# Nearest 2x upsampling on one core: the last of three loads grows from 6 to 8 KB per partition, and SyncE instead of GpSimd ends the program

## The chip, the cores and the metric

The kernel runs on one core of one Trainium2 chip. The time is device time in microseconds (us), lower is better. Beside it stands the *span* of a profile, which goes from the start of the first to the end of the last of the program's own instructions; every timed run has both. The profile calls VectorE DVE, ScalarE ACT, GpSimd POOL, TensorE PE and SyncE SP. Engines and DMAs report progress by *semaphores*, counters that other engines wait for; a DMA has *landed* when its last semaphore step has been made. All runs quoted were at a granted clock of 1.0. A ratio is the mean time of one kernel's runs over that of the other's of the same rounds, so it is not quite the ratio of the medians that stand beside it.

## The reference

```python
batch, channels, h, w = (16, 64, 64, 64)          # float32
result[:, :, i, j] = x[:, :, i // 2, j // 2]      # 128 x 128 out
```

16.78 MB come in, 67.11 MB go out, and there is no arithmetic. Each of the 128 partitions holds 512 rows of 64 floats (128 KB in, 512 KB out).

## The kernel before

Three loads, issued at once by SyncE, bring everything into SBUF. Ten groups of rows are then expanded by VectorE (9/16 of each) and ScalarE, and each group is stored with one DMA.

```python
rows = [40, 44, 44, 54, 54, 56, 56, 56, 56, 52]      # rows per store, sum 512
cuts = [0, R // 2, R - 24, R]                        # loads of 256, 232 and 24 rows
loads = [nc.sync.dma_start(out=xt[:, lo:hi], in_=xp[:, lo:hi])
         for lo, hi in zip(cuts, cuts[1:])]
...
for n, k in enumerate(rows):
    ...
    nc.vector.tensor_copy(out=u[:, :kv], in_=expanded(r0, r0 + kv))
    nc.scalar.copy(out=u[:, kv:], in_=expanded(r0 + kv, r0 + k))
    store = nc.sync.dma_start(out=op[:, r0 : r0 + k, :], in_=u)
    if n == 0:
        tc.add_manual_dep(store.ins, loads[-2].ins.name, ...,
                          reason="stores begin as the loads end")
```

The first store needs only rows of the first load, but is held until the second load (`loads[-2]`) has landed. A row is 256 bytes per partition, so the loads are 64, 58 and 6 KB per partition. Each value is written four times, so a store of 56 rows has 56 KB per partition. In the trace every DMA is 128 data packets, one for each partition, and each of the 16 DMA engines moves eight of them: load packets are 64, 58 and 6 KB here, store packets 40 to 56 KB.

The end of the program was already rearranged. GpSimd (POOL in the profile) waits for all landings, the last store's included, clears the semaphores, and only then releases the other engines:

```python
blocks[-1].instructions = others + [
    d0, gather0, release0, gather1, d1, landed, clear, d2, release1
]
```

Of the kernel before, what the change touches and what calls it, by code (L numbers as in the profile page):

```python
# [1 line left out]

# [4 lines left out]



EARLY = 1  # L10


def begin_before_barrier(nc):



    blocks = nc.main_func.blocks
    main, body = blocks[0], blocks[1]
    sp = mybir.EngineType.SP
    loads = [i for i in body.instructions if i.engine == sp][:EARLY]  # L20
    for load in loads:
        assert isinstance(load, mybir.InstDMACopy), type(load)
        assert not (load.sync_info and load.sync_info.on_wait)
    names = [i.name for i in loads]
    body.instructions = [i for i in body.instructions if i.name not in names]
    kept = list(main.instructions)
    at = next(
        n
        for n, i in enumerate(kept)
        if i.engine == sp and isinstance(i, mybir.InstDrain)  # L30
    )
    kept[at:at] = loads
    main.instructions = kept


def close_on_gpsimd(nc):



    blocks = nc.main_func.blocks  # L40
    sp, pool = mybir.EngineType.SP, mybir.EngineType.Pool
    stores = [
        i
        for i in blocks[1].instructions
        if i.engine == sp and isinstance(i, mybir.InstDMACopy)
    ]
    last = stores[-1].sync_info.on_update[0].id

    end = list(blocks[-1].instructions)
    wait = end[0]  # L50
    assert wait.engine == sp and isinstance(wait, mybir.InstDrain)
    waits = sorted(wait.sync_info.on_wait, key=lambda w: w.id != last)
    assert waits[0].id == last and len(waits) > 2

    mine = [i for i in end if i.engine == pool]
    kinds = [type(i).__name__ for i in mine]
    assert kinds == [
        "InstDrain",
        "InstEventSemaphore",
        "InstEventSemaphore",  # L60
        "InstDrain",
        "InstISA",
        "InstDrain",
        "InstEventSemaphore",
        "InstEventSemaphore",
    ], kinds
    d0, gather0, release0, d1, clear, d2, gather1, release1 = mine
    landed = mybir.InstDrain(
        name=wait.name,
        engine=pool,  # L70
        debug=wait.debug,
        sync_info=mybir.SyncInfo(on_wait=waits, on_update=[]),
    )
    others = [i for i in end if i.engine != pool and i is not wait]
    blocks[-1].instructions = others + [
        d0, gather0, release0, gather1, d1, landed, clear, d2, release1
    ]


@with_exitstack  # L80
def kernel(
    ctx: ExitStack,
    tc: tile.TileContext,
    x: bass.AP,
    scale_factor: int,
    out: bass.AP,
):
    nc = tc.nc
    nc.at_finalize(begin_before_barrier)
    nc.at_finalize(close_on_gpsimd)  # L90
    P = nc.NUM_PARTITIONS
    s = int(scale_factor)
    B, C, H, W = x.shape
    R = B * C * H // P
    fdt = x.dtype



    xp = x.rearrange("b c h w -> (b c h) w").rearrange("(p r) w -> p r w", p=P)
    op = out.rearrange("b c (h hd) w -> (b c h) (hd w)", hd=s).rearrange(  # L100
        "(p r) w -> p r w", p=P
    )




    rows = [40, 44, 44, 54, 54, 56, 56, 56, 56, 52]
    GROW = s * s
    FREE = 79
    WF = FREE * GROW * W  # L110
    assert sum(rows) == R
    mem_pool = ctx.enter_context(tc.tile_pool(name="mem", bufs=1))
    mem = mem_pool.tile([P, WF + R * W], fdt, name="mem")
    xt = mem[:, WF:].rearrange("p (r w) -> p r w", r=R)



    cuts = [0, R // 2, R - 24, R]
    loads = [
        nc.sync.dma_start(out=xt[:, lo:hi], in_=xp[:, lo:hi])  # L120
        for lo, hi in zip(cuts, cuts[1:])
    ]

    def expanded(r0, r1):
        return (
            xt[:, r0:r1].unsqueeze(2).unsqueeze(4).to_broadcast([P, r1 - r0, s, W, s])
        )

    r0 = 0
    before = (0, 0)  # L130
    for n, k in enumerate(rows):
        size = k * GROW * W
        at = 0 if n % 2 == 0 else WF + r0 * W - size
        assert at >= before[1] or at + size <= before[0]
        before = (at, at + size)
        u = mem[:, at : at + size].rearrange(
            "p (k a w b) -> p k a w b", k=k, a=s, w=W
        )
        kv = k * 9 // 16
# [4 lines that stand above are left out]
            tc.add_manual_dep(  # L144
                store.ins,
                loads[-2].ins.name,
                mybir.DependencyInfo(
                    mybir.DependencyClass.Sync, mybir.DependencyReason.DATA
                ),
                reason="stores begin as the loads end",  # L150
            )
        r0 += k


# [1 line left out]
_INS = ['x', 'scale_factor']  # L156
_OUTS = [((16, 64, 128, 128), 'float32')]

_NUMBERS = {'scale_factor': 2}


# [26 lines left out]
```

## Time and profile before

| | before |
|---|---|
| median time | 198.72 us (198.65 to 198.76, 6 runs) |
| span of the profiled run | 196.92 us |
| time minus span | 1.78 us |
| DMA engines holding a packet | 99.0% of the span |
| DVE, ACT busy | 30%, 26% |
| last data packet ends | 196.20 us |
| last store's last semaphore step ("last landing") | 196.54 us |

The DMA engines are full and the compute engines mostly wait for buffers; the chain of waits is made of DMA to 71%. The last two rows come from the trace's packet and semaphore records. Those records do not name a packet's DMA engine; where this text speaks of one engine, packets were paired that follow one another within a few ns.

### The profile page before, as it was taken

To read this page: it belongs to the slowest core of one execution; us is meant where nothing else is said; L and a number is where in the kernel's file an instruction comes from. 1 tells how busy PE (TensorE), PEld (TensorE's weight loads), DVE (VectorE), ACT (ScalarE), POOL (GpSimd) and SP (SyncE) were. 2 spreads that over 40 slices of the span, in tenths; PEclk is the share of its full clock that TensorE was granted. 3 is DMA by queue.
4 is the path that set the end of the run, shared out by engine and by line. 5 is a ranking of instruction groups with operands and counts; after the bars stand their busy time and mean duration, and the time that the engine had idled before them with its cause. 6 is when DMAs were issued, how large, how long until landed. Compare 5 with 4: busy or idle time off the path is not lost.

```text
span 196.9 us, 104 instructions
## 1 busy us (share of the span) xinstructions
DVE 59.6 (30%) x10; ACT 52.1 (26%) x11; POOL 0.2 (0%) x4
## 2 busy tenths in 40 slices
DVE  0000570000050340610393096059119506900000
ACT  2000591000170360695000093800019460000000
POOL 0000000000000000000000000000000000000000
DMA  9999889699999999998989989889989989989995
GB/s 426 426 426 426 386 386 567 274 490 399 413 439 439 439 439 439 461 438 359 539 359 483 422 373 547 384 373 524 408 373 478 454 373 443 489 373 457 422 443 249
DMA packets 1872, 83.89 MB, mean 426 GB/s; under 512 B 208, under 2 KB 208, under 8 KB 336
## 3 DMA queue, kind: packets, MB, share of 16 engines
q1 hardware_dynamic: 1872, 83.89, 99.0%
HBM read 16.78 MB, written 67.11 MB: 426 GB/s over the span
## 4 chain that ended last, share of the span: by engine, by line
DMA 71%; DVE 13%; ACT 3%; issue 0%; SPq 0%; DVEq 0%; ACTq 0%
DMA out_dram<-mem 51%; DMA mem<-in_x_dram 20%; DVE mem L140 13%; ACT mem L141 3%; SPq L142 0%; DVEq L140 0%; ACTq L141 0%
## 5 line engine op out<-in xcount | busy, mean ns | idle before, releaser
L140 DVE COPY mem<-mem 128x7936 f32<-128x7936 f32 (+4 forms) x10 | 59.6, 5969 | 112.2 <-DMA out_dram<-mem 90.4
L141 ACT COPY mem<-mem 128x6400 f32<-128x6400 f32 (+4 forms) x10 | 50.8, 5077 | 107.8 <-DMA out_dram<-mem 81.8
L141 ACT ACT_TABLE_LOAD x1 | 1.3, 1283 | 0.8 <-PEq L169 0.8
L169 POOL MEMSET const-bfloat16-1.0<- 128x1 bf16 x1 | 0.1, 101 | 0.0
L169 POOL MEMSET const-uint8-127<- 128x1 uint8 x1 | 0.1, 101 | 0.0
L169 POOL MEMSET const-float32-0.0<- 128x1 f32 x1 | 0.1, 98 | 0.2 <-issue 0.2
L169 POOL MEMSET const-float32-1.0<- 128x1 f32 x1 | 0.1, 98 | 0.0
## 6 DMA issues: line engine op xcount, KB each, us to landing
out_dram<-mem SPq DMA_DIRECT2D x4, 7168.0 KB, 25.3
out_dram<-mem SPq DMA_DIRECT2D x2, 6912.0 KB, 25.8
out_dram<-mem SPq DMA_DIRECT2D x2, 5632.0 KB, 24.6
mem<-in_x_dram SPq DMA_DIRECT2D x1, 7424.0 KB, 38.6
out_dram<-mem SPq DMA_DIRECT2D x1, 6656.0 KB, 24.6
out_dram<-mem SPq DMA_DIRECT2D x1, 5120.0 KB, 14.1
mem<-in_x_dram SPq DMA_DIRECT2D x1, 768.0 KB, 40.1
mem<-in_x_dram SPq DMA_DIRECT2D x1, 21.9
```

What stands on the lines that cost most here:

```text
L140: nc.vector.tensor_copy(out=u[:, :kv], in_=expanded(r0, r0 + kv))
L141: nc.scalar.copy(out=u[:, kv:], in_=expanded(r0 + kv, r0 + k))
L169: nc = _bacc.Bacc("TRN2", target_bir_lowering=False, num_devices=1)
```

## The change

The intent is to give the DMA queue its first store before it runs dry, by letting the load that releases it land sooner, and to leave as little as possible to do after the last store's landing.

```diff
-    cuts = [0, R // 2, R - 24, R]
+    cuts = [0, R // 2, R - 32, R]
...
-    nc.at_finalize(close_on_gpsimd)
+    nc.at_finalize(close_early)
```

and in the new `close_early` (cut to its core, with `InstDrain` and `InstEventSemaphore` shortened):

```diff
+    lo, hi = clear.ant_dict["range_first"], clear.ant_dict["range_last"]
+    clears = []
+    for a, b in ((lo, last), (last + 1, hi + 1)):       # all but the last store's semaphore
+        if a < b:
+            clears.append(nc.gpsimd.sem_clear(range(a, b)).ins)
...
+    landed = InstDrain(engine=pool, on_wait=[w for w in waits if w.id != last])
+    final = InstEventSemaphore(engine=sp, on_wait=[w], on_update=[subtract w.wait_value])
-        d0, gather0, release0, gather1, d1, landed, clear, d2, release1
+        d0, gather0, release0, gather1, release1, d1, landed, *clears, d2, final
```

More of the change, by code (lines that the diff above doesn't have):

```diff
@@ L77, in close_on_gpsimd, with close_early @@
     ]
+def close_early(nc):
+    blocks = nc.main_func.blocks
+    sp, pool = mybir.EngineType.SP, mybir.EngineType.Pool
+    stores = [
+        i
+        for i in blocks[1].instructions
+        if i.engine == sp and isinstance(i, mybir.InstDMACopy)
+    ]
+    last = stores[-1].sync_info.on_update[0].id
+    end = list(blocks[-1].instructions)
+    wait = end[0]
+    assert wait.engine == sp and isinstance(wait, mybir.InstDrain)
+    waits = list(wait.sync_info.on_wait)
+    assert len({w.id for w in waits}) == len(waits) > 2
+    assert all(w.wait_mode == "sem-ge-imm" for w in waits)
+    mine = [i for i in end if i.engine == pool]
+    kinds = [type(i).__name__ for i in mine]
+    assert kinds == [
+        "InstDrain",
+        "InstEventSemaphore",
+        "InstEventSemaphore",
+        "InstDrain",
+        "InstISA",
+        "InstDrain",
+        "InstEventSemaphore",
+        "InstEventSemaphore",
+    ], kinds
+    d0, gather0, release0, d1, clear, d2, gather1, release1 = mine
+    lo, hi = clear.ant_dict["range_first"], clear.ant_dict["range_last"]
+    assert lo <= last <= hi and all(lo <= w.id <= hi for w in waits)
+    clears = []
+    for a, b in ((lo, last), (last + 1, hi + 1)):
+        if a < b:
+            clears.append(nc.gpsimd.sem_clear(range(a, b)).ins)
+    landed = mybir.InstDrain(
+        name=wait.name,
+        engine=pool,
+        debug=wait.debug,
+        sync_info=mybir.SyncInfo(
+            on_wait=[w for w in waits if w.id != last], on_update=[]
+        ),
+    )
+    (w,) = [w for w in waits if w.id == last]
+    final = mybir.InstEventSemaphore(
+        name=clear.name,
+        engine=sp,
+        debug=wait.debug,
+        sync_info=mybir.SyncInfo(
+            on_wait=[w],
+            on_update=[
+                mybir.SyncUpdate(
+                    sync_type=w.sync_type,
+                    id=w.id,
+                    ant_name=w.ant_name,
+                    update_mode="sem-sub-imm",
+                    update_value=w.wait_value,
+                )
+            ],
+        ),
+    )
+    others = [i for i in end if i.engine != pool and i is not wait]
+    blocks[-1].instructions = others + [
+        d0, gather0, release0, gather1, release1, d1, landed, *clears, d2, final
+    ]
 @with_exitstack
```

## The prediction

> **What bounds the kernel now.** I read the page first: busy shares, the slices of DMA, the chain of waits. DVE is busy for 30% of the span and ACT for 26%, so neither is the bound; the DMA row is.
>
> ```profile
> span 196.9 us, 104 instructions
> DMA  9999889699999999998989989889989989989995
> ...
> q1 hardware_dynamic: 1872, 83.89, 99.0%
> HBM read 16.78 MB, written 67.11 MB: 426 GB/s over the span
> ```
>
> The reader is to see that the 16 DMA engines hold a packet for 99.0% of their time. 83.89 MB have to move whatever the kernel does, and the change moves exactly the same bytes in the same number of packets. What is left to win is the 1% in which the engines are not moving data, so I looked for that: at the start, at the turn from loads to stores, and at the end. The windows view shows the start (first two lines below), the turn (third line), and the long middle.
>
> ```profile
> 0.00:1.00 1.00, 0.00 (x0) 0.21 (x1) 0.20 (x4) 1.00 0.00 0
> 1.00:1.48 0.48, 0.00 (x0) 0.48 (x1) 0.00 (x0) 1.00 6.52 2185
> ...
> 40.48:41.05 0.57, 0.00 (x0) 0.00 (x0) 0.00 (x0) 1.00 2.74 1161
> ...
> 42.00:180.00 138.00, 53.24 (x8) 42.28 (x8) 0.00 (x0) 1.00 1.00 433
> ```
>
> The columns are the stretch, its length, busy time of DVE, ACT and POOL, the granted clock, the DMA share and GB/s; packets are counted where they start. From 42 to 180 us the share is 1.00 at 433 GB/s: no room there. At the start no packet begins before 1.00 us, and all 16 engines begin between 1.00 and 1.48. The first load was issued at 0.00, so **issue to first packet is 1.00 us on idle engines**. The change does not touch that.
>
> The turn is in the chain of waits in order of time (start, length, what):
>
> ```profile
> 0.79 38.60 DMA mem<-in_x_dram
> ...
> 39.41 0.03 SPq L142
> 39.44 0.05 issue
> 39.49 0.35 SPq L142
> ```
>
> The 58-row load, second of three, lands at 39.40; SyncE passes the wait and issues the first store at 39.49. By the 1.00 us above, the earliest store packet is due at 40.49, and the trace's packet records have the first at 40.487, the last engine's first at 41.04. In the same records the 16 engines end the 6 KB load packets between 40.30 and 40.88. Pairing ends with starts in sorted order, every engine stands empty for 0.15 to 0.20 us, on average 0.17. Between loads, and between all the later stores, the same records show 2 to 3 ns. So this is the only hole between the first packet and the last.
>
> The end is in the view of the program's closing line:
>
> ```profile
> L183 POOLq DRAIN  x2: 34/34/34, 196.6 to 196.8; - x2
> L183 POOLq EVENT_SEMAPHORE_RANGE_CLEAR  x1: 93/93/93, 196.6 to 196.6; - x1
> L183 POOLq EVENT_SEMAPHORE  x1: 17/17/17, 196.8 to 196.8; - x1
> ...
> L183 PEldq EVENT_SEMAPHORE  x1: 51/51/51, 196.9 to 196.9; - x1
> ```
>
> Numbers after the count are nanoseconds. The records put the last data packet's end at 196.20 and the last semaphore step of the last store at 196.54. Then follow in series on POOL a drain (34 ns), the clear (93), a drain (34) and the release (17), with gaps of about 25 to 40 ns, and the release wait of the other engines (PE's takes 51). The span ends at 196.92: **0.38 us of bookkeeping after the last landing**.
>
> **What the Trainium skill says.** "DMA: Bandwidth & Descriptors", section "Where 436 GB/s comes from", puts the ceiling of the 16 ports at 435.2 GB/s; the middle runs at 433, which agrees and says that only holes can be removed. The same page, "Latency and other measured facts", gives about 600 ns to the first byte of a DMA issued from SyncE; this trace has 1.00 us from the issue's start, so I use 1.00. "Trace Analysis", section "Per-instruction lifecycle: what the profiler-reported window actually captures", says that for sequencer instructions the profiled window leaves out the semaphore wait and its propagation; this agrees with the gaps of 25 to 40 ns that stand between the closing instructions. "Runtime: NRT & Kernel Launch", section "The ~15µs preamble/postamble breakdown", has a barrier and a reset of semaphores after the kernel's own instructions. The profiled run took 198.7 us and its span 196.9, so 1.8 us lie outside what the trace shows me; some of it may be such work.
>
> **The change part by part.** (1) *The split of the loads.* The second load shrinks from 58 to 56 KB per partition, the last grows from 6 to 8 KB. Each engine has 8 packets of each. A 6 KB packet follows the one before by 230.7 ns in the records; 8 KB should take 230.7 + 2048 / 27.2 bytes per ns (the slope between the 58 KB and the 64 KB packet: 6144 bytes in about 226 ns) = 306 ns. Eight of them: 2.45 us instead of 1.85. So the landing that releases the store comes 0.60 us sooner, at about 38.80, the issue at 38.89, and the earliest store packet at 39.89 instead of 40.49, while the last load still ends on each engine between 40.30 and 40.88. The store's packets are then queued before the engines run out, by 0.4 us on the first. If lateness of the issue makes the hole, it closes to 2 ns: **minus 0.17 us**, and as all later stores follow one another without a gap, the end moves by all of it. The order of instructions on each engine is otherwise unchanged: rows 480 to 487 are used by the last group alone, which waited for that load before too.
>
> (2) *The close.* POOL now waits for all landings but the last store's, clears the semaphores on both sides of that one, and is done while the last store still moves. The releases of the other engines go out before. After the last landing there remains one SyncE semaphore instruction that waits and subtracts 32. SyncE's other semaphore waits take 17 to 28 ns and begin some 15 ns after the landing (0.01 to 0.02 us at the first store). So the end comes about 0.04 us after the landing instead of 0.38: **minus 0.34 us**. The extra second clear (about 93 ns) runs on POOL some 15 us before the end (at about 181 us, when the ninth store lands) and is hidden.
>
> Sum: 0.34 sure, 0.17 with a chance that I put at 60%, so 0.10 expected, and a guess of 0.05 for the part outside the span: 198.72 - 0.49 is about **198.2**. The span should go from 196.9 to about 196.4.
>
> **The rivals.** *The hole stays.* For it speaks that it is so even: engines whose load ended 0.6 us apart all lose 0.15 to 0.20, as if turning from reading HBM to writing it had a fixed price. Against it speaks the first store packet, at issue plus 1.00 us to within 0.01, as on idle engines. Then only the close is won: 198.4. *The hidden end gets work too.* Four engines are through 15 us early, so part of the 1.8 us outside the span may overlap with the last store; then up to some 0.4 us more: 197.8. *The close only moves cost.* The barrier after the kernel may be ordered so that SyncE being last costs the steps that POOL's release cost before; then only the hole is won: 198.5. *More overlap of loads with early stores slows both.* All go through one queue in order, so I expect none. *An engine becomes the bound.* The ninth store's landing, about 181, lies 9 us after the last store's issue at 171.9; no compute is near the path.
>
> **Range and chances.** The parts span 198.5 (one part fails) to 197.8 (overlap outside the span). The three runs before lie within 0.11 us, and I allow 0.1 for drift between sessions. Prediction 198.2 us, range 197.9 to 198.5 for 8 in 10. Two per cent would be 4 us; nothing here is a tenth of that in doubt, so faster 0.01, within 2% 0.98, slower 0.01.
>
> **What would show it.** In the changed profile: the second load lands near 38.8 and the first store is issued near 38.9; the first store packets follow the last load's within 10 ns, or again after 0.17 (then the hole is a turnaround). The last landing comes at about 196.37 (196.54 if the hole stays), and the only closing instruction after it is SyncE's, ending 0.03 to 0.05 later. The time minus the span stays 1.8 us, or shrinks if the end overlaps. I am wrong if the stores lose their 2 to 3 ns spacing, if SyncE's closing instruction takes far more than 28 ns, or if time minus span grows by 0.2 or more.

## The result, and the profile after

The changed kernel takes **197.19 us** (median; 197.09 to 197.45, 6 runs) against 198.72, ratio 0.9925 (95% interval 0.9913 to 0.9938). So 1.53 us are won where 0.5 were forecast, and the time lies outside the forecast range. By the 2% measure it counts as the same speed, as forecast.

The page of the changed kernel, the lines that answer to those shown of before:

```profile
span 195.8 us, 105 instructions
DMA  9999889699999999998989989988988988988988
q1 hardware_dynamic: 1872, 83.89, 99.3%
HBM read 16.78 MB, written 67.11 MB: 428 GB/s over the span
```

The slices hardly differ from before, but for the last (8 instead of 5). That digit is mostly an effect of the edge: a packet counts where it starts, and every engine now starts two inside the last slice, while before most engines started the first of these just ahead of it. Such slices are almost 5 us wide and cannot show what happened here.

The chain of waits in order of time (start, length, what) at the turn from loads to stores:

```profile
0.79 37.95 DMA mem<-in_x_dram
...
38.76 0.03 SPq L216
38.79 0.05 issue
38.83 0.35 SPq L216
```

The second load lands at 38.74 and the first store is issued at 38.83 (before: 39.40 and 39.49), as worked out. In the packet records each engine's first store packet now follows its last load packet by 2 to 5 ns instead of 150 to 200.

The view of the program's closing line after 190 us has one row left:

```profile
L257 SPq EVENT_SEMAPHORE  x1: 17/17/17, 195.8 to 195.8; - x1
```

The last landing is at 195.81, the span ends 0.033 us later (before: 0.377).

Both of these came as forecast. Two other things did not. First, the time minus the span fell from 1.78 to 1.32 us in the profiled runs. Second, the last data packet ends 0.75 us sooner, though the hole at the turn was only 0.17. The view in order of time, VectorE only, shows where the rest comes from. Each of these copies starts when a 56-row or 54-row store lands and frees its buffer, so the starts tell the pace of the stores. Before:

```profile
113.12 8.42 DVE L140 COPY mem<-mem 128x7936 f32<-128x7936 f32 x1 [7.95 <-DMA out_dram<-mem]
...
163.97 7.89 DVE L140 COPY mem<-mem 128x7424 f32<-128x7424 f32 x1 [8.52 <-DMA out_dram<-mem]
```

After:

```profile
112.59 8.42 DVE L214 COPY mem<-mem 128x7936 f32<-128x7936 f32 x1 [7.89 <-DMA out_dram<-mem]
129.50 8.42 DVE L214 COPY mem<-mem 128x7936 f32<-128x7936 f32 x1 [8.49 <-DMA out_dram<-mem]
...
163.32 7.89 DVE L214 COPY mem<-mem 128x7424 f32<-128x7424 f32 x1 [8.53 <-DMA out_dram<-mem]
```

From the first to the last of these lines three stores pass: 50.85 us before, 50.73 after. The lead of the changed kernel grows from 0.53 to 0.65 us in a stretch in which both do the same work. The packet records say it outright. *Slow* means here, and below: more than 1 ns longer than the shortest packet of that size in the changed kernel.

| packet | ns before, mean | slow | ns after, mean | slow |
|---|---|---|---|---|
| 40 KB, first store | 1523.9 | 126 of 128 | 1514.0 | 0 of 128 |
| 44 KB | 1671.5 | 225 of 256 | 1665.0 | 0 of 256 |
| 54 KB | 2048.7 | 238 of 256 | 2041.0 | 0 of 256 |
| 56 KB | 2122.6 | 450 of 512 | 2116.3 | 10 of 512 |
| 52 KB | 1970.0 | 109 of 128 | 1966.4 | 2 of 128 |

Eight packets of each store pass through an engine, so the sum is 8 x 9.9 + 16 x 6.5 + 16 x 7.7 + 32 x 6.3 + 8 x 3.6 = 537 ns. (From the engines' first store packets to their last ends, on the average, it is 155.18 us before and 154.65 after, the same 0.53.) The gain of 1.53 us now splits into the hole (0.17), the stores' pace (0.53), the close inside the span (0.34) and the part outside it (0.46); what is left is small and has to do with how far the engines stand apart.

### The profile page after: what moved, and what is told of

Same layout as the page of the kernel before. It is cut to its first block, busy times and chain, and to the rows that moved or that the text cites. A ratio compares the mean times of both kernels' runs of the same rounds, so it can differ in the third digit from the quotient of the medians.

```text
span 195.8 us, 105 instructions
## 1 busy us (share of the span) xinstructions
DVE 59.6 (30%) x10; ACT 52.1 (27%) x11; POOL 0.2 (0%) x4
## 4 chain that ended last, share of the span: by engine, by line
DMA 71%; DVE 13%; ACT 3%; issue 0%; SPq 0%; DVEq 0%; ACTq 0%
DMA out_dram<-mem 52%; DMA mem<-in_x_dram 19%; DVE mem L214 13%; ACT mem L215 3%; SPq L216 0%; DVEq L214 0%; ACTq L215 0%
```

## The experiments

Each kernel is the changed one with the edit shown, gave the correct output, and was timed in rounds shared with the kernel before (five runs where nothing else is said). Where a label says "56 KB packets", the mean of the 512 packets of the four 56-row stores is meant.

### Split alone, and close alone

Which part of the change makes the stores faster, and which the part outside the span? Three theories for the pace: the emptied queue (H), the sizes 56 and 8 KB (S), the new close (C).

```diff
-    nc.at_finalize(close_early)
+    nc.at_finalize(close_on_gpsimd)      # e1: 8 KB split, old close
```

> Undoes the close, keeps the 8 KB split. Where the stores' pace comes from, three theories. H (an emptied queue at the turn slows all later store packets) and S (the sizes 56 and 8 KB do it): no hole at the turn (2 to 3 ns), 56 KB store packets at 2116 ns as in the changed kernel (2122.6 before), last landing near 195.8, plus 0.38 of the old close, span near 196.2. C (the close does it): packets at 2122 to 2123, span near 196.7. Time minus span 1.8 if the close alone is worth the 0.46 outside the span (time 198.0), 1.3 if the split is (time 197.5).

Measured: 198.13 us (197.99 to 198.48) against 198.75, ratio 0.9964 (0.9950 to 0.9977). Time minus span 1.75 to 1.83 in all five runs, as before. The pace lay *between*: 56 KB packets 2119.1 ns, 209 of 512 slow. The profiled run explains why. In it the engines started their loads up to 1.1 us apart, the load that releases the store landed late (issue at 39.16 instead of 38.83), and of 16 engines seven ran dry, for 0.17 us on the average, while the others went on within a few ns. The slowness goes with the single engine: in the first store 54 of the 56 packets of those seven engines are slow and none of the other 72, and in each later store the count stays close to that (48 to 55 of 128).

So 8 KB is only just enough. In the profiles of e7, e8, e9 and e10, shown below, which have that split too, one, one, no and two engines ran dry at the turn, and the first store has 8, 8, 0 and 16 slow packets of 128. But the number grows later on: the last 56 KB store has 28, 57, 4 and 33, though the packet records show no engine pausing for more than 3 ns after the turn. So a dry queue is enough to make an engine slow, but an engine can also become slow without one; by what, no run here shows. Either is a plausible reason for the wider spread of the changed kernel (0.36 us against 0.11), though only the profiled runs show their packets.

```diff
-    cuts = [0, R // 2, R - 32, R]
+    cuts = [0, R // 2, R - 24, R]        # e2: 6 KB split, new close
```

> Keeps the new close, back to the 6 KB split. H and S: a hole of about 0.17 at the turn, 56 KB store packets at 2122 to 2123 ns, last landing near 196.5, span near 196.6; time minus span 1.3 if that belongs to the close, so time 197.9. C: packets at 2116, span near 196.05, time 197.4.

Measured: 197.94 us (197.86 to 198.03), ratio 0.9957 (0.9945 to 0.9970). The first store was issued at 39.41, the 56 KB packets took 2122.6 ns, the span was 196.53 and time minus span 1.33 to 1.36. So the close has no part in the pace (C falls), and the 0.45 us outside the span belong to the close. With the 0.34 inside it, the close alone is worth about 0.8 us.

### A longer hole, and no hole at the old sizes

```diff
-    cuts = [0, R // 2, R - 32, R]
+    cuts = [0, R // 2, R - 16, R]        # e3: last load of 4 KB
...
-        if n == 0:
+        if n <= 1:                       # keeps the stores in order
```

> New close, last load of 4 KB, so the queue should stand empty longer, about 0.17 + 0.60 = 0.77 us (the second store is tied to the same landing, to keep the order of the stores). H: store packets slow, 2122 ns or more, span near 197.2, time 198.5; if the slowdown grows with the hole, more than 2125 ns. S says nothing of 4 KB. If the hole and the pace are unrelated, packets at 2116, span 196.6, time 197.9.

Measured: 198.14 us (197.97 to 198.17), ratio 0.9965 (0.9952 to 0.9977). Issue at 40.05; all engines' first store packets began between 40.89 and 41.04, so the hole was 0.40 us on the average (0.19 to 0.65 if the engines are paired in order), less than the 0.77 that I expected: here the first packets came 0.84 us after the issue, not 1.00, and the engines started together. The 56 KB packets took 2122.6 ns, to the tenth what they took after a hole of 0.17. Between these two sizes of hole, the slowdown does not grow.

```diff
-    cuts = [0, R // 2, R - 32, R]
+    cuts = [0, R // 2, R - 24, R]        # e4: old sizes ...
-                loads[-2].ins.name,
+                loads[0].ins.name,       # ... and the first store not held
```

> New close, 6 KB split, but the first store isn't held for the second load: it is issued as soon as its copies are done (about 26 us) and queues behind the loads. No hole. H: store packets at 2116, span near 195.85, time 197.2, as the changed kernel. S: packets at 2122 to 2123 in spite of the full queue, span near 196.4, time 197.7. If early stores disturb the loads, 58 KB load packets take more than 2192 ns and the time is over 197.7.

Measured: 198.46 us (198.38 to 198.63), ratio 0.9985 (0.9972 to 0.9997). All but 4 of the 1,280 store packets had the fast length (56 KB: 2116.1 ns, 2 of 512 slow), with the sizes of the kernel before. S falls, H stands. The time was bad all the same: the loads suffered. The 58 KB packets took 2227 ns on the average instead of 2192 and the 6 KB packets 337 instead of 234, nearly all of the excess from about 34 us on. The page's list of issues shows it in the landing (bytes, then us from issue to landing; the last two of the three loads):

```profile
mem<-in_x_dram SPq DMA_DIRECT2D x1, 7424.0 KB, 39.2
mem<-in_x_dram SPq DMA_DIRECT2D x1, 768.0 KB, 41.3
```

Before, the same two took 38.6 and 40.1. So the loads lost more than a microsecond. Against e2, which differs by the hold alone, the time is 0.52 us longer, although the hole and the slow stores are gone. The first store must not be queued too late, but not too early either.

### How early is too early

```diff
-    cuts = [0, R // 2, R - 32, R]
+    cuts = [0, R // 2, R - 40, R]        # e5: 10 KB;  e6: R - 64, 16 KB;  e11: R - 36, 9 KB
```

> Changed kernel with a last load of 10 KB: the first store is issued another 0.6 us sooner (near 38.2). If the spread of the changed kernel's times (197.09 to 197.45) comes of engines that still run dry in some runs, as half of them did in the split-only run, no engine runs dry here: 56 KB store packets at 2116 ns in every profile, time 197.1 with a spread under 0.2. If a store issued too early disturbs the loads, as the store without hold did (58 KB load packets at 2227 ns), the last load's packets take over 390 ns (some 384 without) and the time is over 197.4.

Measured: 197.46 us (197.31 to 197.68), ratio 0.9935 (0.9924 to 0.9947). No dry engine, 56 KB packets at 2116.1 ns. But 25 of the 128 packets of the last load were slowed, from 39.07 on, some 0.9 us after the store's issue at 38.17: mean 405 ns instead of 385, which is 0.16 us on an engine.

> Changed kernel with a last load of 16 KB, the first store issued some 2.4 us sooner than in the changed kernel (near 36.4). If the harm of the store without hold comes of being queued some 4 us before the loads end, the last load's packets are slowed (over 620 ns against some 609) and the time is 197.4 to 198.4; if it needs the 14 us of that run, no slowing and 197.1.

Measured: 198.45 us (198.22 to 198.71), ratio 0.9984 (0.9972 to 0.9996). Store issued at 36.44; the last load's packets slow from about 38.0 on, mean 732 ns instead of 611, which is 0.97 us on an engine. All but 4 of the 1,280 store packets are fast. The last load landed late:

```profile
mem<-in_x_dram SPq DMA_DIRECT2D x1, 6144.0 KB, 35.6
mem<-in_x_dram SPq DMA_DIRECT2D x1, 2048.0 KB, 41.0
```

> Changed kernel with a last load of 9 KB, between 8 KB (some engines still run dry in some runs) and 10 KB (none dry, but the last load's packets slowed, 0.16 us lost on an engine). If both effects meet in between, no engine dry, packets of the last load slowed by less than 0.1 us on an engine, 56 KB store packets at 2116, time 197.1 to 197.3. If the dry queue is rare at 8 KB, 9 KB is no better than 197.19.

Measured: 197.38 us (197.34 to 197.41, 4 runs), ratio 0.9930 (0.9916 to 0.9945). No dry engine (56 KB packets 2116.2) and no slowed load packet (all 347 ns). Its spread is a fifth of that of 8 KB, but its median is no better; in the profiled run one engine began its stores 0.36 us after the next-last and so ended last. 8 and 9 KB cannot be told apart by these runs: their intervals overlap for the most part.

### Which engine ends the program

The part outside the span fell by 0.45 us with the new close. My rival in the prediction had a reason for such a gain: four engines are through early. A different one is that the engine that ends last brings its own tail.

```diff
-            on_wait=[w for w in waits if w.id != last], on_update=[]
+            on_wait=sorted(waits, key=lambda w: w.id != last), on_update=[]
...
-        d0, gather0, release0, gather1, release1, d1, landed, *clears, d2, final
+        d0, gather0, release0, gather1, release1, d1, landed, clear, d2     # e7
```

> 8 KB split; the other engines are released early as in the change, but POOL waits for the last store and clears all semaphores after it, so POOL ends the program. Span: last landing plus 0.25 to 0.30 (drain, clear, drain), so 196.05 to 196.1 with a full queue. The 0.45 us outside the span: if they come of the four other engines being through early, time minus span is 1.34 and the time 197.4; if they come of SyncE being last in POOL's place, it is 1.79 and the time 197.9.

Measured: 198.05 us (197.88 to 198.79, 6 runs), ratio 0.9970 (0.9957 to 0.9982). The closing view shows the three instructions on POOL that are left after the landing, 0.242 us in all:

```profile
L232 POOLq DRAIN  x2: 34/34/34, 196.0 to 196.2; - x2
L232 POOLq EVENT_SEMAPHORE_RANGE_CLEAR  x1: 93/93/93, 196.1 to 196.1; - x1
```

Time minus span was 1.81 to 1.89, although all other engines had been through for 24 us (their release is at 172.3). So the early release is worth nothing; what counts is which engine is last. In the kernel before, POOL's last instruction ends 0.09 us before the span (then the other engines pass their release), so from POOL's end to the end of the time there were 1.78 + 0.09 = 1.87 us: the same tail.

```diff
-        engine=sp,
+        engine=mybir.EngineType.Activation,     # e8;  e9: DVE;  e10: PE
```

> The changed kernel, but the last wait and subtraction on ACT, so ACT ends the program. If only the early release of the others counts, time minus span 1.34 and the time 197.2 as the changed kernel; if SyncE is special, 1.5 to 1.8 and 197.4 to 197.7.

> Changed kernel, DVE in place of SyncE makes the last wait and subtraction. Theory E: what lies outside the span is a tail that belongs to the engine that ends last (SyncE 1.34, ACT 1.51, POOL 1.86 so far). Then time minus span is a constant of DVE's own, whatever its size, to within 0.05 over the runs; under the rival, that SyncE is special and all others pay what the barrier costs, it is 1.5 or more. Span as the changed kernel, 195.8 to 196.2.

> The same with PE as the last engine. Its semaphore instructions take 51 ns where SyncE's take 17, so the span grows by about 0.03. Theory E: time minus span a constant of PE's own; if it is under 1.28, this kernel beats the changed one. Rival: 1.5 or more.

Measured, with SyncE and POOL beside them:

| last engine | time minus span, us, all runs | median time |
|---|---|---|
| SyncE (changed kernel) | 1.29 to 1.36 | 197.19 |
| DVE (e9, 4 runs) | 1.42 to 1.49 | 197.37 (197.25 to 197.52), ratio 0.9933 |
| ACT (e8) | 1.48 to 1.54 | 197.44 (197.41 to 197.79), ratio 0.9938 |
| PE (e10, 4 runs) | 1.62 to 1.69 | 197.56 (197.52 to 197.94), ratio 0.9944 |
| POOL (e7) | 1.81 to 1.89 | 198.05 (197.88 to 198.79), ratio 0.9970 |

The spans are given to 0.1 us, so each value can be off by 0.05; in the profiled runs, with exact spans, the five are 1.32, 1.46, 1.50, 1.68 and 1.85. Each engine has a tail of its own, which the trace does not show, and SyncE's is the shortest. (POOL's is the only one measured with the clearing of the semaphores just before it; POOL with the bare wait and subtraction was not tried.) That SyncE is alone in having a small one, my rival, is wrong: DVE's is 0.1 longer and no more. None of the three beats the changed kernel.

### A dry queue away from the turn

H had been tested only where loads and stores meet. The last kernel makes the queue run dry once in the middle of the stores:

```diff
+        if n == 5:                        # the sixth store waits for the fifth one's landing
+            tc.add_manual_dep(store.ins, stored.ins.name, ...)
+        stored = store
```

> Changed kernel, but the sixth store (the first of 56 KB) waits for the fifth one's landing, so every engine's queue runs dry once, in the middle of the stores, with no load near. Theory D (a queue that has run dry leaves its engine with slower packets from then on): packets of the first five stores at 1514, 1665 and 2041 ns as in the changed kernel, all 56 KB packets after the hole at 2122 to 2123 and the 52 KB ones at 1970; the hole of some 1.3 us (0.35 to the landing, 1.0 from issue to first packet) and 5 stores by about 0.05 us each, so span near 197.4 and time 198.7. Rival T (only a late turn from loads to stores does it): 56 KB packets stay at 2116, span near 197.1, time 198.5.

Measured: 199.06 us (198.90 to 199.26, 4 runs) against 198.84, ratio 1.0013 (0.9996 to 1.0030). Two lines around the hole, from the view in order of time of VectorE:

```profile
112.75 8.42 DVE L214 COPY mem<-mem 128x7936 f32<-128x7936 f32 x1 [7.87 <-DMA out_dram<-mem]
131.16 8.42 DVE L214 COPY mem<-mem 128x7936 f32<-128x7936 f32 x1 [10.00 <-DMA out_dram<-mem]
```

The second copy starts 18.41 us after the first, against 16.9 in the changed kernel: that is the hole. In the packet records the engines end the fifth store between 111.71 and 112.30 us and begin the sixth between 113.53 and 113.68, so each stands empty for 1.64 us on the average. Ahead of it the packets are fast (40, 44, 54 KB: 1514.6, 1665.4, 2041.5 ns, with 39 of 640 slow, 8 in the first store: one engine ran dry at the turn). After it, the four stores of 56 KB average 2128.6, 2123.5, 2124.0 and 2123.1 ns and the 52 KB one 1970.4. The sizes, the close and the turn are those of the changed kernel; only the hole is new. The hole was longer than I had allowed for, though, 1.64 us instead of 1.3: span 197.73 instead of 197.4.

## Why the prediction was wrong, point by point

- **The split of the loads: right, with its mechanism, but with no room to spare.** An 8 KB packet was to follow the one before by 306 ns; it did (each took 309 in the records, and the next began some 3 ns before its end). Issue at 38.89 was forecast, 38.83 came; the hole fell from 0.17 us to 2 to 5 ns. But the 0.4 us in hand, counted from 1.00 us after the issue, were not there: in e1 seven engines ran dry although they ended their loads only 1.35 to 1.45 us after the issue. In the changed kernel's profile the first engine ended them 1.52 us after it. That no engine ran dry there was in part luck: of the seven profiles with this split, two have no dry engine (this and e9), e7, e8 and e12 one, e10 two and e1 seven. The rival "the hole stays", a fixed price of the turn, is refuted by the changed kernel and by the store without hold. That the hole had looked so even spoke for the wrong side.
- **The close inside the span: right.** 0.34 us forecast, 0.344 came (0.377 to 0.033).
- **The step that failed first** is "no room there", said of the stretch from 42 to 180 us because its share was 1.00 at 433 GB/s, and with it the assumption that the end moves by just the hole. It was missing a term: a dry queue slows the packets after it. That term measured 0.53 us, three times the hole itself. Nothing in the windows view could have told: it counts packets where they start, so a packet more or less at an edge moves it by about 1% (the fast 16 KB run shows 432 GB/s for 112 to 180 us, the kernel before 433). What did show it already before is the spread of packets of one size: the 58 KB load packets of that kernel stayed within 4 ns of one another (2192 to 2196), the first store's spread over 1514 to 1551. I had both in the records and asked of neither why.
- **The term that was mis-sized** is the 0.05 us for the part outside the span; it measured 0.46. The rival that named up to 0.4 more gave the wrong reason: engines that are through early win nothing (1.81 to 1.89 with POOL last). What wins is that POOL's tail of about 1.87 us (0.09 of it inside the span) is exchanged for SyncE's of about 1.32. The opposite rival, that the barrier after the kernel makes SyncE pay what POOL paid, is refuted by the same table.
- **The sum.** 0.17 + 0.53 + 0.34 + 0.46 = 1.50, of which the prediction had 0.10 (after weighing the hole at 60%), nothing, 0.34 and 0.05. The measured gain is 1.53. The remaining 0.03 to 0.05 comes from how far the slowest engine stands behind the mean (0.31 us before, 0.19 after at the last packet, against loads that ended 0.07 later on the average), which changes from run to run.
- **No transfer slowed another**, as forecast, holds for 8 and 9 KB only. From 10 KB on the early store slows the last load, by a mechanism that I had ruled out because all goes through one queue in order.

What stays open: why an engine whose queue has run dry handles most of its packets 4 to 10 ns slower for the rest of the program (the runs show that it does, with three lengths of hole, at two places; no record shows how), why some engines become slow later without having run dry, and what the tails consist of. I did not try a way to make a dry engine fast again.

## What to carry to other kernels

In a kernel that is bound by DMA, keep the queue from ever running dry: the hole was worth 0.17 us, its after-effect on the later packets 0.53. But don't queue a store far ahead of the end of the loads; here a last load of 8 KB was sometimes too late and one of 10 KB already too early. In these profiles engines ran dry that ended their loads up to 1.48 us after the first store's issue, and none that ended them later; with 10 KB, where the first engine ended them 2.21 us after it, load packets were slowed. And let the engine with the shortest tail be the last one: the time has a part that no profile shows, and comparing time minus span over a few variants measures it.

## What the Trainium skill lacked or had wrong

- "DMA: Bandwidth & Descriptors" (and no other page that I read) says nothing of packets that are slower after the queue has run dry: 56 KB store packets of 2122.6 ns instead of 2116.1 to 2116.3, over the rest of the program, for a hole of 0.17 or of 0.40 us, and 2123 to 2129 ns after a hole amid the stores.
- The same page, "Rules for kernel authors", advises to issue a DMA early so that its fixed cost overlaps. It lacks the limit: a store queued behind loads slows them. Last load's packets 405 ns instead of 385 (10 KB), 732 instead of 611 (16 KB), 337 instead of 234 (not held, 6 KB), up to 1.3 us of time over the 8 KB split.
- The same page, "Latency and other measured facts", has about 600 ns to the first byte for a DMA issued by SyncE. It does not say from when it counts. From the start of the issuing instruction these runs have 1.00 us on idle engines (0.62 from its end), and 0.84 us (0.50) where the queue ran dry for 0.40 us.
- "Runtime: NRT & Kernel Launch", section "The ~15µs preamble/postamble breakdown", has a barrier and resets after the kernel, but not that what follows depends on the engine that ends last: time minus span of 1.29 to 1.36 us with SyncE, 1.42 to 1.49 with DVE, 1.48 to 1.54 with ACT, 1.62 to 1.69 with PE, 1.81 to 1.89 with POOL.
